# A hybrid decoder layer on one core: the pairwise recurrence, scores and value products as products of the whole array

## The chip, the core and the metric

The kernel runs on one core of a Trainium2 chip. Its time is the device time of one execution in microseconds, and the median of three runs is given. TensorE is the matrix engine, VectorE and ScalarE the vector engines, POOL (GpSimd) and SP two more, of which SP issues most of the transfers here.

## What is computed

One layer for 512 tokens of width 2048 in float32. The token's vector is normalized and multiplied with `w_in` (7296 columns); three groups of heads work on the result, each is gated with a SiLU, and one output projection adds to the input. Cut to what matters:

```
proj = _rms(x, norm_g) @ w_in                    # split into pa, pb, pc
# A: 12 heads of 64, a recurrence over the tokens
sa    = einsum('bhvk,bhk->bhv', state, -kk_t)
state = state * w_t + sa * (kk_t * a_t) + v_t * k_t
y_t   = einsum('bhvk,bhk->bhv', state, r_t)
# B: trailing means over 2, 4, 8 and 16 tokens minus the token, then a 128 x 128 map
yb = einsum('bsgc,gcd->bsgd', mean - u, pool_w) * pool_scale * silu(pg)
# C: 12 heads of 64, stick-breaking attention, strictly causal
z = q k^T;  log_1m = log_sigmoid(-z);  w = exp(log_sigmoid(z) + sum of the later log_1m)
yc = (w @ v) * silu(gc)
out = x + concat(ya, yb, yc) @ w_out
```

## The kernel before

**Projections.** `w_in` is cut into 57 tiles of 128 columns (`tile_order`): one for the decay and rate inputs, then for each of six pairs of heads eight tiles (k, r, v, ga of the recurrence, cq, ck, cv, cg of the attention), then eight for the pooling. A float32 product is made of three in the faster format f32r, of high and low parts (`three`, L408): 16 blocks x 3 = 48 products of 128x128 by 512 tokens per tile, into one of two banks `pj`. The weights come in halves of a tile, are split by ScalarE (`wh`) and VectorE (`wl`), and VectorE evacuates the result (`u`). The first three tiles run while the input arrives (`first`). The output projection at the end has 4 x 16 x 4 x 3 = 768 products (`oacc`).

**Small work in between.** All else is written as generators (`rwkv`, `attention`, `pooling`). After each big product `pump` lets those go on whose inputs are ready by a clock that `Pace` keeps while the program is built. `need(..., tag, margin)` gives that time. So the order on TensorE is fixed beforehand, and a wrong estimate becomes a wait. On VectorE, ScalarE and POOL the operations run in program order, weights and evacuations being put ahead (L426, L447).

**The recurrence** (`rwkv`, L506) treats two heads, one in the upper and one in the lower 64 rows, in eight chunks of 64 tokens. A pair waits until the pair before is done (L558). Then come the products inside the chunks (`gm`, L581 to L593, 64 rows of one head at a time), a triangular solve on VectorE by way of DRAM (L598 to L635), two visits of 32-row products (`q`) that complete the inverse `lt`, and the chunk loop from L687:

- `w`: two products of 128 rows and 64 columns, one for each head; VectorE copies the result to `wsb` and makes the decayed state `se`.
- `y`: two products of 64x64 (L702); `u`: two of 64x64 with `lt` (L705); VectorE copies u into `uv`.
- `s`: two products with `bkt`, then VectorE's update of `uv` for the next chunk with `se`; `y` again with `rx`, and ScalarE copies y out.

These are plain float32 products, and each stands as two records in the trace. Banks of PSUM are dealt out by kind: two for `pj`, three `g`, three `c`.

**The attention** (`attention`, L739) makes the scores `z` of a head in four blocks. In each block one product of 128 rows (high and low part of q against the high part of k) is followed by one of 64 rows (`klo`, L778). ScalarE, VectorE and POOL make the weights `w` of it, TensorE transposes them (`wT`), and four products per head, 64 columns wide, multiply with the values (`o`, L831). Decay and rate (`dec`, `av`, L519 to L525) are also a product of 128 rows and one of 64.

**Pooling** (L839) waits with its product until the last pair's recurrence and attention are through (L859), and the output projection takes the branches in the order recurrence, attention, pooling (`order`, L939).

Of the kernel before, what the change touches and what calls it, by code (L numbers as in the profile page):

```python
# [8 lines left out]
F32 = mybir.dt.float32  # L9
# [4 lines left out]
P = 128  # L14
# [38 lines left out]
BANKS = {"pj": 2, "g": 3, "c": 3}  # L53
# [150 lines left out]
def hybrid_trunk_kernel(ctx: ExitStack, tc: tile.TileContext, x, xT, w_in, w_out, vecs, consts, up_w, pool_w, out, tap=None):  # L204
# [15 lines left out]
    tp = ctx.enter_context(tc.tile_pool(name="tp", bufs=14))  # L220
# [57 lines left out]

    hh = [hp.tile([P, T], F32R, tag=f"hh{k}", name=f"hh{k}") for k in range(KT)]
# [14 lines left out]
    for pl, tag, parts in ((ap, "q2", 1), (ap, "k2", 1), (ap, "w3", 1), (rp, "bk", 2), (rp, "bkt", 2), (rp, "rx", 2),  # L294
                           (rp, "uv", 2), (rp, "amr", 3), (ap, "wt", 2)):
        xt = pl.tile([P, parts, T], F32, tag=tag, name=name("x"))
# [209 lines left out]
    def rwkv(p):  # L506
# [13 lines left out]
        mm(dec, upl[lo, 0:P], wd2[lo, :], False, True)  # L520
# [4 lines left out]
        mm(av, upl[hi, P:2 * P], ad2[hi, :], False, True)  # L525
# [35 lines left out]
        amr = rp.tile([P, NC_, 3, C], F32, tag="amr", name=name("amr"))  # L561
        for h, s in ((0, lo), (1, hi)):
# [7 lines left out]
        dve.tensor_tensor(amr[:, :, 2, :], r3, e[:, :, 1:], ALU.mult)  # L570
# [7 lines left out]
        lt = rp.tile([P, NC_, C], F32, tag="lt", name=name("lt"))  # L578
        ms = strict.rearrange("p (o t) -> p o t", o=1)
        mi = incl.rearrange("p (o t) -> p o t", o=1)  # L580
        for half in range(2):  # L581
            cs = slice(4 * half, 4 * half + 4)
            for h, s, other in quad:
                yield need(*([amr, bk] if half == 0 and h == 0 else []), tag="g")
# [6 lines left out]
                dve.tensor_tensor(lt[s, cs, :], g4[s, :, 0, :], ms[s].to_broadcast([HD, 4, C]), ALU.mult)  # L591
# [6 lines left out]
        for h in range(2):  # L598
            for b in range(2):
                r0 = h * HD + b * B  # L600
                dma(out=s1v[:, :, h, b, :], in_=lt[r0:r0 + B, :, b * B:(b + 1) * B])
# [30 lines left out]
        for h in range(2):  # L632
            for b in range(2):
                r0 = h * HD + b * B
                dma(out=lt[r0:r0 + B, :, b * B:(b + 1) * B], in_=s2v[:, :, h, b, :])  # L635
# [23 lines left out]
        xt = tmp("xt")  # L659
        dve.transpose(xt, lt.rearrange("p c t -> p (c t)"))  # L660
# [391 lines left out]
```

## Time and profile before

| | us |
|---|---|
| median of 3 runs | 1089.75 (1088.41 to 1089.97) |
| the profiled execution | 1089.68 |
| its span, first to last instruction | 1088.0 |
| TensorE busy | 1066.2 (98%) |
| VectorE busy | 737.6 (68%) |
| ScalarE busy | 427.8 (39%) |
| POOL busy | 143.1 (13%) |

In the rows PE is TensorE's product, DVE is VectorE, ACT is ScalarE. Products are pipelined: one begins before the one ahead of it has ended, so what one costs is read from start to start and not from its own length. A tile's name stands without its number, as out<-in. Ahead of a product's sizes stand the rows and columns of the array that it uses (128*128 is the whole of it).

### The profile page before, as it was taken

The page shows a single profiled execution, that of the slowest core. Times are in us where ns is not written, and L with a number is a line of the kernel's source. Part 1 is how long each engine was busy: PE and PEld are TensorE (multiplying, and loading weights), DVE is VectorE, ACT ScalarE, POOL GpSimd, SP SyncE. Part 2 cuts the span into 40 slices and gives each one's busy share as a digit, 9 for nine tenths or more (in the row PEclk, how much of TensorE's full clock was granted, in tenths as well). Part 3 has the DMA queues.
Part 4 walks back from the last instruction along what each step waited for, and adds up shares of the span by engine and source line. Part 5 has one row for each costly group of instructions (what it writes and reads, how often), then busy time and mean ns, then how long its engine had stood idle before and what let it go on. Part 6 is the DMA issues. An engine that isn't in the chain of part 4 may idle for free.

```text
span 1088.0 us, 14731 instructions
## 1 busy us (share of the span) xinstructions
PE 1066.2 (98%) x5552; PEld 801.3 (74%) x5552; DVE 737.6 (68%) x1596; ACT 427.8 (39%) x670; POOL 143.1 (13%) x208
## 2 busy tenths in 40 slices
PE   9998999999999999999999999999999999999998
PEld 7877766687666877668766787667776677888887
DVE  6266978759787797778877799777986457223232
ACT  6453525235353354334543345524443235111111
POOL 0031113101132011210211102210021111000000
PEclk9999999999999999899999999999999999999999
DMA  9513231132211321113221132112221125444232
GB/s 329 204 63 105 80 93 40 56 92 84 84 48 51 107 85 66 58 59 97 86 76 39 64 115 77 61 58 84 100 78 55 48 94 163 149 154 137 96 137 75
DMA packets 58185, 101.92 MB, mean 94 GB/s; under 512 B 29312, under 2 KB 30720, under 8 KB 58112
## 3 DMA queue, kind: packets, MB, share of 16 engines
q1 hardware_dynamic: 58112, 100.96, 28.2%
q8 instruction: 44, 0.72, 0.3%
q14 instruction: 29, 0.24, 0.1%
HBM read 95.17 MB, written 5.77 MB: 93 GB/s over the span
## 4 chain that ended last, share of the span: by engine, by line
PE 80%; DVE 10%; issue 4%; ACT 2%; DMA 2%; POOL 2%; SPq 0%; POOLq 0%; DVEq 0%; ACTq 0%
PE pj L350 45%; PE oacc L350 15%; PE first L350 3%; PE o L350 2%; PE z L350 2%; DVE w L198 2%; DVE wl L198 2%; PE gm L350 2%; PE y L350 2%; PE w L350 2%; PE wT L354 1%; DVE xblk L198 1%; PE u L350 1%; POOL e L198 1%; PE s L350 1%
## 5 line engine op out<-in xcount | busy, mean ns | idle before, releaser
L350 PE MATMUL pj<-hl,wh 128*128 128x512 f32 x864 | 349.0, 404 | 0.0
L350 PE MATMUL pj<-hh,wh 128*128 128x512 f32 x864 | 347.9, 403 | 1.0 <-DVE u L198 0.8
L350 PE MATMUL pj<-hh,wl 128*128 128x512 f32 x864 | 347.6, 402 | 0.0
L198 DVE TENSOR_TENSOR wl<-raw,wh 128x1024 fp32r<-128x1024 f32 x140 | 172.1, 1229 | 168.6 <-ACT wh L198 162.8
L198 ACT CAST wh<-raw 128x1024 fp32r<-128x1024 f32 x140 | 147.0, 1050 | 312.7 <-PE pj L350 187.5
L350 PEld LDWEIGHTS pj<-hh,wh 128*128 128x128 f32 x864 | 163.1, 189 | 38.0 <-issue 4.4
L350 PEld LDWEIGHTS pj<-hh,wl 128*128 128x128 f32 x864 | 163.2, 189 | 35.4 <-issue 0.4
L350 PEld LDWEIGHTS pj<-hl,wh 128*128 128x128 f32 x864 | 163.1, 189 | 35.5 <-issue 1.2
L350 PE MATMUL oacc<-wl,yh 128*128 128x512 f32 x256 | 100.1, 391 | 0.8 <-DVE wl L198 0.8
L350 PE MATMUL oacc<-wh,yl 128*128 128x512 f32 x256 | 99.6, 389 | 0.0
L350 PE MATMUL oacc<-wh,yh 128*128 128x512 f32 x256 | 99.6, 389 | 0.0
L198 POOL TENSOR_SCALAR e<-e 128x512 f32<-128x512 f32 x28 | 49.0, 1749 | 327.9 <-ACT e L198 327.6
L198 POOL TENSOR_TENSOR d<-u 128x512 f32<-128x512 f32 x25 | 34.2, 1370 | 230.9 <-DVE u L198 148.6
L350 PEld LDWEIGHTS oacc<-wl,yh 128*128 128x128 f32 x256 | 48.0, 188 | 11.5 <-DVE wl L198 1.3
L350 PEld LDWEIGHTS oacc<-wh,yl 128*128 128x128 f32 x256 | 48.1, 188 | 10.0 <-issue 0.2
L350 PEld LDWEIGHTS oacc<-wh,yh 128*128 128x128 f32 x256 | 48.0, 188 | 10.0
L198 DVE TENSOR_TENSOR xblk<-xblk,pr 128x60 f32<-128x60 f32 (+8 forms) x180 | 44.5, 247 | 4.1
L198 ACT ACTIVATE e<-e 128x512 f32<-128x512 f32 x50 | 31.4, 629 | 39.1 <-POOL e L198 38.8
L198 DVE TENSOR_TENSOR_SCAN w<-kon,n 128x512 f32<-128x512 f32 (+3 forms) x48 | 39.3, 841 | 6.6 <-POOL n L198 6.5
L198 DVE TENSOR_TENSOR pr<-xblk,nblk 128x60 f32<-128x60 f32 (+8 forms) x180 | 38.7, 215 | 4.4
L198 DVE TENSOR_TENSOR u<-pj,rstd 128x512 f32<-128x512 f32 x50 | 34.3, 686 | 8.3 <-PE pj L350 7.9
L198 ACT ACTIVATE n<-n 128x512 f32<-128x512 f32 (+1 forms) x72 | 38.9, 557 | 1.3
(195 smaller groups left out, 1262.7 us busy)
## 6 DMA issues: line engine op xcount, KB each, us to landing
raw<-in_w_in SPq DMA_DIRECT2D x108, 512.0 KB, 3.4
raw<-in_w_out SPq DMA_DIRECT2D x32, 512.0 KB, 3.4
xs<-in_x SPq DMA_DIRECT2D x8, 512.0 KB, 4.7
xr<-in_x SPq DMA_DIRECT2D x16, 256.0 KB, 5.3
out<-xr SPq DMA_DIRECT2D x16, 256.0 KB, 3.2
fr<-in_w_in SPq DMA_DIRECT2D x12, 256.0 KB, 7.4
nblk<-s SPq DMA_DIRECT2D x24, 128.0 KB, 4.9
x<-in_xT SPq DMA_DIRECT2D x5, 512.0 KB, 7.4
```

Source lines behind the costliest of these rows:

```text
L198: return call(*args, **kw)
L350: pe.matmul(o, lhsT, rhs, start=start, stop=stop)
L354: pe.transpose(o, src, ident)
```

## The change

Every product of the recurrence becomes one of the whole array: `amr` gets four columns per chunk (two for each head) and `lt` two, and the halves of the other head are set to zero, so that both heads go in one product and the wanted halves are picked out behind it. The copy of `w` is then two copies, y of four chunks gathers in a bank of its own, and `se` moves from VectorE to POOL. Scores, decay and rate use 128 rows throughout; for the scores POOL makes `kl2`, the low part of k twice. The value products of both heads of a pair are made side by side in one bank. Pooling doesn't wait any more, and the output projection takes pair 5 last. `tp` has 13 buffers instead of 14.

```diff
-BANKS = {"pj": 2, "g": 3, "c": 3}
+BANKS = {"pj": 2, "g": 3, "c": 2, "y": 1}
+Y_ORDER = [0, 1, 2, 3, 4, 10, 11, 12, 13, 14, 6, 7, 8, 9, 5, 15]
...
-            c = max(4 * max(n, 64) / 2400.0, 0.1) * (0.6 if m <= 64 or rhs.shape[0] <= 64 else 1.0)
+            c = max(4 * max(n, 64) / 2400.0, 0.214 if m > 64 else 0.1) * (0.6 if m <= 64 or rhs.shape[0] <= 64 else 1.0)
...
-        mm(dec, upl[lo, 0:P], wd2[lo, :], False, True)
+        mm(dec, upl[:, 0:P], wd2, False, True)
...
-        for h, s in ((0, lo), (1, hi)):
+        for h, s, other in quad:
+            pool.memset(amr[other, :, h, :], 0.0)
...
-        dve.tensor_tensor(amr[:, :, 2, :], r3, e[:, :, 1:], ALU.mult)
+        dve.tensor_tensor(amr[lo, :, 2, :], r3[lo], e[lo, :, 1:], ALU.mult)
+        pool.tensor_tensor(amr[hi, :, 3, :], r3[hi], e[hi, :, 1:], ALU.mult)
...
-                    rhs = amr[s, cc, 0:3:2, :] if h == 0 else amr[s, cc, 1:3, :]
-                    mm(g[:, j * P:(j + 1) * P], bk[s, cc, :, :], rhs)
+                    mm(g[:, j * P:(j + 1) * P], bk[:, cc, :, :], amr[:, cc, h:4:2, :])
...
-            yield need(amr, uv, tag="c", margin=TIGHT)
-            wps = cb("w")
-            for h, s, o in quad:
-                mm(wps[s, 0:C], amr[:, cc, h, :], uv[:, cc, h, :])
+            yield need(amr_flat, uv, tag="c", margin=TIGHT)
+            wus = cb("wus")
+            wps, ups, sps = wus[:, 0:P], wus[:, P:P + C], wus[:, 2 * P:3 * P]
+            mm(wps, amr[:, cc, 0:2, :], uv[:, cc, :, :])
             wsb = rp.tile([P, C], F32, tag="wsb", bufs=2, name=name("wsb"))
-            dve.tensor_copy(out=wsb, in_=wps[:, 0:C])
+            dve.tensor_copy(out=wsb[lo, :], in_=wps[lo, 0:C])
+            dve.tensor_copy(out=wsb[hi, :], in_=wps[hi, C:P])
...
-                    dve.tensor_scalar(se[s, :], uv[s, cc, h, :], ec[s, cc:cc + 1], None, ALU.mult)
-            yield need(wsb, lt, tag="c", margin=TIGHT)
...
-                mm(yps[s, 0:C], uv[s, cc, h, :], amr[s, cc, 2, :], True, False)
...
-                mm(ups[s, 0:C], lt[s, cc, :], wsb[s, :])
...
+                    pool.tensor_scalar(se[s, :], uv[s, cc, h, :], ec[s, cc:cc + 1], None, ALU.mult)
+            yield need(wsb, lt, tag="y" if cc % 4 == 0 else None, margin=TIGHT)
+            mm(ups, lt[:, cc, :, :], wsb)
...
+            mm(yps, uv[:, cc, :, :], amr[:, cc, 2:4, :], True, False)
+            dve.tensor_copy(out=uv[lo, cc, 0, :], in_=ups[lo, :])
+            dve.tensor_copy(out=uv[hi, cc, 1, :], in_=ups[hi, :])
+            yield need(uv, margin=TIGHT + 0.1)
...
-                    mm(sps[s, 0:C], bkt[:, cc, h * HD:(h + 1) * HD], uv[:, cc, h, :])
+                mm(sps, bkt[:, cc, :], uv[:, cc, :, :])
...
+            mm(yps, uv[:, cc, :, :], rx[:, cc, :, :], False, True)
...
+            kl2 = ap.tile([P, T], F32R, tag="kl2", name=name("kl2"))
+            pool.tensor_copy(out=kl2[s, :], in_=klo[s, :])
+            pool.tensor_copy(out=kl2[other, :], in_=klo[s, :])
...
-                    mm(z[:, off:off + (i + 1) * P], q2[s, i * P:(i + 1) * P], klo[s, 0:(i + 1) * P], False, True)
+                    mm(z[:, off:off + (i + 1) * P], q2[:, i * P:(i + 1) * P], kl2[:, 0:(i + 1) * P], False, True)
...
-            for j in range(4):
-                mm(o[s, j * P:T], vt[:, j, s], wt[:, pos[j]:pos[j] + T - j * P], j == 0, j == 3)
...
+            for j in js:
+                for h, s in ((0, lo), (1, hi)):
+                    mm(o[s, j * P:T], vt[:, j, s], parts[h][:, pos[j]], j == 0, j == 2)
...
-        while ("pg", g) not in got or not done.get(("gn", NPAIR - 1)) or not done.get(("att", NPAIR - 1)):
+        while ("pg", g) not in got:
...
+    for h, s, other in quad:
+        pool.memset(amr[other, :, 2 + h, :], 0.0)
+        pool.memset(lt[s, :, 1 - h, :], 0.0)
...
-    while len(tasks) > 1:
-        pump(True)
...
-        k = order[i]
-        while 6 <= k < 10 and tasks:
+        k = Y_ORDER[i]
+        while not done.get(ready[k]):
             pump(True)
```

## Rows read from the trace of the kernel before

**Rows 1.** Busy us (instructions) of PE, PEld, DVE, ACT, POOL; clock, DMA, GB/s.

```profile
42.00:908.00 866.00, 851.19 (x4619) 624.40 (x4617) 660.95 (x1502) 366.11 (x594) 137.06 (x199) 0.99 0.24 76
485.00:615.00 130.00, 128.77 (x722) 93.94 (x720) 104.42 (x240) 55.52 (x93) 20.24 (x30) 1.00 0.24 75
```

**Rows 2.** Chain of waits (start, us, what), and TensorE's timeline at the first output product.

```profile
920.99 163.28 PE oacc L350 x719
...
908.00 0.39 PE L350 MATMUL oacc<-wh,yh 128*128 128x512 f32 x1
```

**Rows 3.** Timeline of TensorE (start, us, instruction): a visit of u.

```profile
575.50 0.40 PE L350 MATMUL pj<-hh,wh 128*128 128x512 f32 x1
575.83 0.33 PE L350 MATMUL u<-wsb,lt 64*64 64x64 f32 x4
...
576.42 0.40 PE L350 MATMUL pj<-hh,wl 128*128 128x512 f32 x1
```

**Rows 4.** The same view: a visit of s and y, and the second big product behind.

```profile
854.11 0.34 PE L350 MATMUL s<-uv,bkt 128*64 128x64 f32 x4
854.27 0.29 PE L350 MATMUL y<-rx,uv 128*64 128x64 f32 x4
...
854.83 0.40 PE L350 MATMUL pj<-hh,wl 128*128 128x512 f32 x1
```

**Rows 5.** The same view: four transposes, and the two big products behind.

```profile
544.25 0.60 PE L354 MATMUL wT<-kon,w 128*128 128x128 f32 x4
544.60 0.47 PE L350 MATMUL pj<-hl,wh 128*128 128x512 f32 x1
544.91 0.39 PE L350 MATMUL pj<-hh,wl 128*128 128x512 f32 x1
```

**Rows 6.** The same view: a pooling product, and the second big product behind.

```profile
885.59 1.02 PE L350 MATMUL po<-pd,pw 128*128 128x512 f32 x2
...
886.68 0.40 PE L350 MATMUL pj<-hh,wl 128*128 128x512 f32 x1
```

**Rows 7.** The same view: the eight score products of a head.

```profile
656.50 0.40 PE L350 MATMUL z<-k,q 128*128 128x512 f32 x1
656.83 0.50 PE L350 MATMUL z<-klo,q 64*128 64x512 f32 x1
...
659.46 0.39 PE L350 MATMUL pj<-hh,wh 128*128 128x512 f32 x1
```

**Rows 8.** The same view: the decay's two products.

```profile
567.36 0.42 PE L350 MATMUL dec<-wd,sh 128*128 128x512 f32 x1
567.71 0.49 PE L350 MATMUL dec<-wd,sl 64*128 64x512 f32 x1
568.13 0.50 PE L350 MATMUL pj<-hh,wh 128*128 128x512 f32 x1
```

**Rows 9.** Chain of waits: first products of pair 3, and of pair 4.

```profile
485.31 1.64 PE gm L350 x16
488.54 1.08 PE gm L350 x8
...
615.15 1.64 PE gm L350 x16
```

**Rows 10.** Timeline of TensorE: the value products of a head.

```profile
553.02 2.37 PE L350 MATMUL o<-wt,vt 128*64 128x512 f32 x8
```

**Rows 11.** The same view: a visit of 32-row products.

```profile
547.29 0.69 PE L350 MATMUL q<-xt,lt 32*32 32x32 f32 x32
```

**Rows 12.** VectorE's groups of 485 to 615 us: count, busy us, mean ns, idle before.

```profile
L198 DVE TENSOR_SCALAR se<-uv,ec 64x64 f32<-64x64 f32 x14 | 3.5, 249 | 0.4
L198 DVE COPY wsb<-w 128x64 f32<-128x64 f32 x8 | 1.8, 223 | 3.6 <-PE w L350 3.4
```

**Rows 13.** The page's costliest groups: POOL.

```profile
L198 POOL TENSOR_SCALAR e<-e 128x512 f32<-128x512 f32 x28 | 49.0, 1749 | 327.9 <-ACT e L198 327.6
```

**Rows 14.** TensorE's waits by releaser: total us, times, longest.

```profile
PE w L350 <- DVE uv L198: 4.2, 5, 1.2
```

More of the change, by code (lines that the diff above doesn't have):

```diff
@@ L583, in rwkv @@
             for h, s, other in quad:
-                yield need(*([amr, bk] if half == 0 and h == 0 else []), tag="g")
+                yield need(*([amr_flat, bk] if half == 0 and h == 0 else []), tag="g")
                 g = gb("gm")
@@ L656, in rwkv @@
         yield soon(lt)
-        xt = tmp("xt")
-        dve.transpose(xt, lt.rearrange("p c t -> p (c t)"))
-        xt3 = xt.rearrange("p (c t) -> p c t", t=C)
+        xt = tmp("xt", NC_ * B)
+        xt3 = xt.rearrange("p (c t) -> p c t", t=B)
+        for h in range(2):
+            dve.transpose(xt3[h * HD:h * HD + B], lt[h * HD:h * HD + B, :, h, 0:B])
         yield need(xt, tag="g")
@@ L812, in attention @@
                 act.copy(out=vt, in_=vps.rearrange("p (j c) -> p j c", j=4))
-            wt = ap.tile([P, 1280], F32, tag="wt", name=name("wt"))
-            pos = {}
-            off = 0
-            for js, width in (((0,), 512), ((1, 3), 512), ((2,), 256)):
-                yield need(*blocks.values(), tag="g", margin=MARGIN + 2.0)
+        o = None
+        for js, width in (((0,), 512), ((1, 3), 512), ((2,), 256)):
+            parts = []
+            for h in range(2):
+                yield need(*head[h].values(), tag="g", margin=MARGIN + 2.0)
                 tps = gb("wT")
-                o2 = 0
+                pos = {}
+                off = 0
                 for j in js:
-                    pos[j] = off + o2
+                    pos[j] = slice(off, off + T - j * P)
                     for i in range(j, 4):
-                        transpose(tps[:, o2:o2 + P], blocks[(i, j)])
-                        o2 += P
-                dst = wt[:, off:off + width]
-                (dve.tensor_copy if js[0] != 1 else act.copy)(out=dst, in_=tps[:, 0:width])
-                off += width
-            yield need(wt, vt, tag="g")
-            o = gb("o")
-            for j in range(4):
-                mm(o[s, j * P:T], vt[:, j, s], wt[:, pos[j]:pos[j] + T - j * P], j == 0, j == 3)
-            while ("cg", p) not in got:
-                yield None
-            y = yt[Y_TILE[("c", p)]]
-            dve.tensor_tensor(y[s, :], o[s, :], y[s, :], ALU.mult)
+                        transpose(tps[:, off:off + P], head[h][(i, j)])
+                        off += P
+                home = {(0, 0): "q2", (0, 1): "k2", (1, 0): "kl2", (2, 0): "q2", (2, 1): "k2"}.get((js[0], h))
+                wt = ap.tile([P, T], F32, tag=home, name=name("wt"))[:, 0:width] if home else tmp("wt", width)
+                (dve.tensor_copy if h == 0 else act.copy)(out=wt, in_=tps[:, 0:width])
+                parts.append(wt)
+            yield need(*parts, vt, tag="g" if o is None else None)
+            if o is None:
+                o = gb("o")
+            for j in js:
+                for h, s in ((0, lo), (1, hi)):
+                    mm(o[s, j * P:T], vt[:, j, s], parts[h][:, pos[j]], j == 0, j == 2)
+        while ("cg", p) not in got:
+            yield None
+        y = yt[Y_TILE[("c", p)]]
+        dve.tensor_tensor(y, o, y, ALU.mult)
         done[("att", p)] = True
@@ L900, in finish @@
             got[(kind, i)] = u
-    first = [cb("first") for _ in range(NFIRST)]
+    first = [bank(("c", "c", "y")[n], "first") for n in range(NFIRST)]
     for kq in range(KT // KQ):
@@ L967, in hybrid_trunk_kernel @@
                 for i in (2 * i2, 2 * i2 + 1):
[L968 removed]
+                    k = Y_ORDER[i]
                     sl = slice((i % 2) * 512, (i % 2) * 512 + 512)
```

66 lines of the change are left out of this document (32 added, 34 removed).

## The prediction

> **What bounds the kernel now.** I read the table of busy time by stretch first. From 42 to 908 us, where all but the first three input columns are projected, TensorE is busy 851.2 of 866 us at a granted clock of 0.99, and VectorE 661 [rows 1]. Waiting is 14.8 us there. So TensorE's own work is the bound, and the question is what that work is. Next the chain of waits: 719 output products in a row took 163.28 us, 0.227 us each [rows 2]. The 54 projected columns have 54 x 16 x 3 = 2592 such products, 588.6 us of the 851.2. The other 262.6 us are the small products that are let in between them.
>
> Then the timeline of TensorE around single visits of small products. I price a visit from the start of the big product ahead of it to the start of the second one behind it, less 2 x 0.227; the ends of products overlap, their starts don't. One fp32 product stands as two records.
> - A visit of four u records: 576.42 - 575.50 - 0.454 = 0.47 us [rows 3]. The lead-in is 0.33 instead of 0.23, and the big product behind has the next one 0.33 after it.
> - s and y together, eight records: 0.72 plus the same lead-in of 0.33, less 0.454, is 0.60 [rows 4]. Four more records cost 0.13, so the first four cost some 0.16 and the remaining 0.3 is the edge of the visit. Four records of 64 columns one after the other at two cycles a column would be 0.21; 0.13 means that the two heads, on different columns of the array, run together.
> - Four 128x128 transposes: 0.66 + 0.23 - 0.454 = 0.44, that is 0.11 each and no edge [rows 5]. One fp32 product 128x128 by 512 columns, two records: 1.09 + 0.23 - 0.454 = 0.87, that is 0.43 each, just the two cycles a column, and no edge either [rows 6].
> - Eight score products, alternately of 128 and 64 rows: 2.96 + 0.24 - 0.454 = 2.75 us for 2560 columns, which stream in 1.07 [rows 7]. Eight changes of shape, about 0.2 each. The decay product has the same: the 64-row half begins 0.35 after the 128-row one and is followed after 0.42, where 0.23 is normal [rows 8].
>
> So the edge is not paid for small fp32 products but each time the shape of the array (rows x columns, the figure ahead of the sizes) changes: some 0.15 to 0.2 us per change. [...]
>
> **The change, part by part.** First what the recurrence costs now, as the remainder of the 262.6 us. Scores 12 x 2.75 = 33.0. The first products of the recurrence (gm): per pair one visit of 16 records at 1.64 and two of 8 at 1.08 [rows 9], each with 0.2 of edge, 4.4 a pair, 26.5. Value products (o): 2.30 of streaming (1280 columns at four cycles are 2.13) and an edge of 0.2, 2.5 per head, 30 [rows 10]. Decay and rate products 12 x 0.88 = 10.5. Transposes 216 x 0.11 = 23.8. The 32-row products (q) 0.69 and edges, 0.9 a visit, 12 visits, 10.9 [rows 11]. 72 other full-shape products at 0.235, 16.9. Pooling 2.6. Together 154, which leaves 108 for the recurrence, 2.25 us a chunk. At its best a chunk has 0.47 + 0.60 + 0.60 = 1.67 or 80 in all; many visits are split in two and pay the edge twice.
> - *Recurrence in full shape.* 5 x 48 - 6 = 234 products in place of 468 in quadrants or halves. Each has two records of 128x128; the rows of that size cost 0.11, so 0.22 a product and 52 to 54 in all. The u product has only 64 moving columns and may cost half: down to 47. Edge: none. Saved: 55 by the remainder, 27 by the best visits; I take 50, near the remainder, which counts what really ran.
> - *Scores with 128 rows.* Eight products at 0.227, 0.174, 0.12 and (as the transposes) 0.11, two of each, 1.27 in place of 2.75: 12 x 1.48 = 18 saved. Decay and rate: 12 x 0.42 = 5 saved.
> - *gm in full shape.* 96 products at 0.22 are 21 in place of 26.5: 5 saved.
> - *Paired value products.* The visits become three per pair, of both heads, with an edge of about 0.3 each. If the heads overlap as in [rows 4], in order of issue the second record of the first head runs with the first of the second: three quarters of the serial time, (1280 x 2 x 4 cycles = 4.27) to 3.1; with edges 4.1 a pair, 24.5 in place of 30, 5 saved. Bounds: no overlap, 1 lost; perfect overlap, 11 saved.
> - *VectorE and POOL.* The copy wsb becomes two (8 x 0.22 more a pair), se goes to POOL (14 x 0.25 less) [rows 12]. VectorE falls from 104.4 to some 102 us a pair. POOL gets se, two copies of klo per head, half of r times E and two clears of half a tile: by its row of 1.75 us for 512 columns [rows 13] at most 4 x 1.75 + 1.75 + 14 x 0.3 + 1.2, or 14 us a pair on top of 20 of 130. It stays mostly idle.
> - *Waits.* The saved edges also covered the hand-over to VectorE. There are 3 x 48 - 6 = 138 hand-overs; late by 0.2 each they cost 28, not late at all 0. At present the longest group of them costs 4.2 us in all [rows 14]. I take 7.
> - *At no cost.* Pooling at once and the last pair last: no product of TensorE is added, and 719 output products follow without a break now [rows 2], so there is no hole to close. They are cover: pair 5 is needed only 14 x 12 x 0.227 = 38 us into the output projection, and if pair 5 comes later than that the rest is paid in full. Ten loads of x instead of nine and four clears of zeros lie in the first 42 us; 0 to 1 us, taken as 0.
>
> The sum: 50 + 18 + 5 + 5 + 5 = 83 saved, 7 given back, 76 in all. The profiled execution took 1089.68 us (span 1088.0 and 1.7 around it), which is the median of 1089.75 within 0.1. So 1089.7 - 83 + 7 = 1013.7, and as u may be cheaper than 0.22 I say 1012.
>
> **The rivals.**
> *A, VectorE becomes the bound.* It is busy 104.4 of the 130 us of a pair, 80% [rows 1]; with 102 of 116 it would be 88%, in strict order, and what it is late with (weights, evacuations) stops TensorE. For: of its 25.6 idle us a pair some come from waiting in order, which a faster TensorE doesn't remove. Against: TensorE waits for it only a few us in all [rows 14]. If 20 of the 25.6 stay, a pair takes 122 and not 116: 6 x 6 = 36 more, of which the waits above hold a part, about 1045.
> *B, the edge belongs to the visit, not to the shape.* Then 144 visits of the recurrence and 18 of gm still pay 0.2 each, 32 us, and the packing of [rows 4] is lost as well: about 1044. Transposes and the pooling product, small or fp32 and without edge, speak against it [rows 5, 6]. [...]
> *C, slower: the chain of a pair grows.* From one pair's gm to the next's are 129.84 us [rows 9], just what eight projected columns take, and the pairs follow one another without overlap there. The change puts se on POOL, in order, behind operations of 1.75 us [rows 13]; VectorE's update of uv waits for it, and everything queued behind that update on VectorE (wl, the evacuations) with it. Pair 5's gm would come at 615 + 130 = 745 and its end by 875 to 885 if the chain stays as long; TensorE, whose output projection begins at 908 now [rows 2], would need it at 908 - 83 + 38 = 863. So an unchanged chain costs 12 to 22, inside the range. To eat the whole gain it must be 10 us longer a pair, 1.3 us a chunk: from there on it is slower, at 2 us a chunk 1089.7 - 76 + 6 x 16 + 15 = 1125. Against: the chunk has some 7 us, and se is needed only at its end.
> *D, no change:* the products are not made full-shape after all or waits take all. The edits leave little room for that.
>
> **How the numbers follow.** Forecast 1012, as worked out: 0.66, with 992 to 1028 as its own range (u at half, 6; perfect overlap, 6; no waits, 7; against it 21 more waits or 7 of value products). A 0.21, B 0.06, C 0.04, D 0.03. All but C and D are faster. For 8 in 10 the range reaches from 992 into most of A: 992 to 1042. Faster by over 0.2% (about what a measurement of this kernel can tell from no change): 0.93; within: 0.03; slower: 0.04.
>
> **What would show it.** Right, if small fp32 products stand as 128*128 in the timeline and the big ones around them keep 0.23 ahead and some 0.3 behind; if the eight scores take some 1.3 us; if TensorE's busy time from 42 us to the first output product falls from 851 to about 770 and VectorE's stays near 655. Value products of two heads should start within each other's time. A shows as TensorE waiting for wl, u or uv for over 30 us; B as lead-ins of 0.33 ahead of 128*128 records; C as a hole in TensorE ahead of the last two of sixteen blocks of the first output columns. The forecast is wrong if a 128x128 fp32 product with 128 columns costs much more than 0.22, or if the remainder of 108 holds something else than the recurrence.

## The result, and the profile after

The changed kernel takes 1100.1 us, median of four runs (1098.6 to 1101.2), the kernel before beside it 1089.9: a ratio of 1.0088, 95% interval 1.0059 to 1.0116. It is slower by 0.9%; forecast were 1012 us. The profiled execution spans 1096.9 us.

The page of the profile after: span, and the busy time of the engines with their shares.

```profile
span 1096.9 us, 13928 instructions
...
PE 1023.6 (93%) x5084; PEld 812.4 (74%) x5084; DVE 726.8 (66%) x1554; ACT 427.8 (39%) x652; POOL 234.7 (21%) x338
```

The table by stretch, whose columns are those of [rows 1], for the time from the first product behind the three input columns to the first output product, and for two windows of the length of a pair.

```profile
40.00:917.00 877.00, 809.57 (x4150) 636.30 (x4149) 650.43 (x1460) 366.22 (x578) 226.11 (x323) 0.97 0.23 75
485.00:615.00 130.00, 122.04 (x634) 94.95 (x633) 101.19 (x231) 53.59 (x85) 34.78 (x50) 0.97 0.23 75
615.00:745.00 130.00, 117.21 (x620) 92.16 (x619) 99.44 (x229) 54.45 (x87) 34.34 (x50) 0.97 0.21 68
```

TensorE is busy 809.6 us where it was 851.2 [rows 1], and yet the stretch is longer, 877 instead of 866: 67 us of it are idle, and the clock fell from 0.99 to 0.97. The output projection takes 180 us in both. So all of the loss lies ahead of it, and the work did become less. Who is waited for stands in TensorE's waits (engine, line, releaser: us in all, times, longest):

```profile
PE q L361 <- DVE xt L201: 21.0, 5, 7.8
PE wus L361 <- DVE uv L201: 12.8, 11, 2.3
PE wus L361 <- DVE wsb L201: 10.1, 10, 2.6
PE q L361 <- DVE w L201: 5.8, 3, 2.8
PE gm L361 <- issue: 5.1, 1, 5.1
```

Nothing like the first line stood in the waits before; their longest group was the 4.2 us of [rows 14]. The wait in pair 4, first in the timeline of TensorE (start, us, instruction, in brackets the idle time ahead of it and its releaser):

```profile
647.25 0.39 PE L361 MATMUL pj<-hh,wl 128*128 128x512 f32 x1
651.94 0.24 PE L361 MATMUL q<-xt,lt 32*32 32x32 f32 x2 [4.30 <-DVE xt L201]
652.11 0.56 PE L361 MATMUL pj<-hh,wh 128*128 128x512 f32 x1
652.47 0.63 PE L361 MATMUL pj<-hl,wh 128*128 128x512 f32 x1
652.89 0.63 PE L361 MATMUL pj<-hh,wl 128*128 128x512 f32 x1
653.32 0.63 PE L361 MATMUL pj<-hh,wh 128*128 128x512 f32 x1
```

and the same wait in the chain of waits (start, us, what):

```profile
612.49 5.96 DMA xblk<-s
...
641.71 0.59 DVE cq L201
642.30 1.14 DVE wl L201
643.90 5.77 DMA s<-xblk
649.68 1.75 DMA lt<-s
651.45 0.44 DVE xt L201
651.94 0.24 PE q L361 x2
```

The 32-row products wait for the triangular solve: 40 us from the load of `xblk` to `q`, in which VectorE's small steps stand between weights (`wl`, 1.14 us) and attention work, and two trips through DRAM. Before, TensorE went from a pair's last `gm` to its `q` in 55.5 us in pairs 2 to 5, with 210 big products between them, and found `xt` ready 2.5 to 2.9 us earlier. In pair 3 of the kernel before, `xt` is done at 544.67, and `q` starts at 547.29 [rows 11]:

```profile
543.97 0.70 DVE L198 STREAM_TRANSPOSE xt<-lt 128x512 f32<-128x512 f32 x1
```

Now the order has 190 to 195 big products there in pairs 3 to 5, and `q` comes after 49.8 to 52.5 us only because it waits. The solve itself, from the last `gm` to `xt`, took 53 us in these pairs before; now it takes 50 to 52 to the first half of `xt`, which is made in two, and 51 to 54 to the whole. It is TensorE that became quicker. The idle time at `q`, as a group of the table by line (count, busy us and mean ns, then idle before, by releaser):

```profile
L361 PE MATMUL q<-xt,lt 32*32 32x32 f32 x192 | 6.2, 214 | 26.3 <-DVE xt L201 21.0 <-DVE w L201 5.3
```

The 5.3 us are of pairs 1 and 2 and aren't the solve's: there `xt` had been ready for 3.4 us, and `q` waited for VectorE's step `w` of the attention, which reads scores from a bank. That it is the bank which `q` needs is likely, not shown.

The chains of the window 615 to 745 us, before and after, in shares of the chain by line:

```profile
by line: PE pj L350 68.7%; PE z L350 3.9%; PE o L350 3.5%; PE gm L350 3.2%; PE y L350 2.6%; PE w L350 2.6%; DVE w L198 2.1%; PE wT L354 1.7%; PE u L350 1.4%; PE s L350 1.2%; POOL e L198 1.2%; PE q L350 1.0%; POOL w L198 0.9%; issue 0.8%; PE
```

```profile
by line: PE pj L361 27.3%; DVE wl L201 6.1%; DVE w L201 6.0%; issue 5.7%; DVE pr L201 5.4%; DVE xblk L201 4.9%; DMA xblk<-s 4.6%; DMA s<-xblk 4.4%; PE gm L361 2.9%; PE wus L361 2.5%; POOL se L201 1.9%; POOL e L201 1.9%; DVE c L201 1.8%; DVE
```

Big products made up two thirds of the chain before and make up a quarter now; the solve (`pr`, `xblk`, `s`) and VectorE's other work have come in.

The idle time isn't all. In the timeline above the big products stand 0.43 us apart behind the wait, where 0.23 is usual. The table by stretch shows the granted clock there, in a stretch almost without waits, and in 17 us around the longest wait (7.8 us, ended at 158.6):

```profile
652.00:655.60 3.60, 3.60 (x12) 2.90 (x12) 3.33 (x6) 0.00 (x0) 0.00 (x0) 0.56 0.47 155
133.00:151.00 18.00, 17.18 (x76) 13.35 (x75) 17.17 (x50) 8.99 (x16) 5.97 (x9) 1.00 0.16 60
154.20:171.20 17.00, 10.78 (x91) 9.06 (x92) 7.23 (x15) 4.78 (x9) 2.27 (x5) 0.50 0.26 76
```

In the traces of before and after every stretch is granted either 1.00 or 0.50, and half clock here means a stretch at 0.50, where the big products stand 0.43 us apart instead of 0.23. In after, every stretch at half clock ahead of the output projection begins in or just behind a wait of 2.5 us or more, and there were 47.8 us of it (10.2 before). Not every wait has one behind it: of the 13 waits of 1.5 us or more, eight have. From here on the stretch up to the first output product is split so: idle time ahead of TensorE's instructions; half of the time at half clock, as lost (an estimate: 0.43 us for 0.23 would be 47%); and the rest, which is TensorE's work at full clock. Idle time that lies at half clock is counted in both of the first two; in after that is 8.1 us, in before none. Without it the work of after is 789.6 and its loss 19.8. One experiment below (se on VectorE, first version) has no such split, since its profiled execution fell into a disturbed run. In us:

| kernel | median | stretch | idle | lost to half clock | rest | idle + rest |
|---|---|---|---|---|---|---|
| before | 1089.9 | 865.9 | 14.8 | 5.1 | 846.0 | 860.8 |
| after | 1100.1 | 876.9 | 67.4 | 23.9 | 785.6 | 853.0 |

TensorE's work fell by 56 to 60 (the first with idle time at half clock taken out); idle time rose by 52.6, and the loss to the clock by 15 to 19.

### The profile page after: what moved, and what is told of

Same layout as the page of the kernel before. It is cut to its first block, busy times and chain, and to the rows that moved or that the text cites. A ratio compares the mean times of both kernels' runs of the same rounds, so it can differ in the third digit from the quotient of the medians.

```text
span 1096.9 us, 13928 instructions
## 1 busy us (share of the span) xinstructions
PE 1023.6 (93%) x5084; PEld 812.4 (74%) x5084; DVE 726.8 (66%) x1554; ACT 427.8 (39%) x652; POOL 234.7 (21%) x338
## 4 chain that ended last, share of the span: by engine, by line
PE 49%; DVE 26%; DMA 10%; POOL 5%; issue 4%; ACT 4%; SPq 1%; POOLq 0%; DVEq 0%; ACTq 0%
PE pj L361 23%; PE oacc L361 15%; DVE wl L201 5%; DVE w L201 3%; DVE xblk L201 3%; DVE pr L201 3%; PE wus L361 3%; DMA s<-xblk 3%; DMA xs<-in_x 2%; PE gm L361 2%; POOL e L201 2%; PE o L361 2%; DMA xblk<-s 2%; DVE u L201 1%; PE y L361 1%
## 5 line engine op out<-in xcount | busy, mean ns | idle before, releaser
L201 DVE TENSOR_TENSOR wl<-raw,wh 128x1024 fp32r<-128x1024 f32 x140 | 176.7, 1262 | 181.5 <-ACT wh L201 180.4
L201 POOL CAST kl<-klo 64x512 fp32r<-64x512 f32 x24 | 18.7, 778 | 236.4 <-DVE klo L201 190.8
L201 POOL TENSOR_SCALAR se<-uv,ec 64x64 f32<-64x64 f32 x84 | 49.8, 593 | 83.9 <-DVE uv L201 79.0
L361 PEld LDWEIGHTS oacc<-wh,yl 128*128 128x128 f32 x256 | 48.0, 188 | 10.2 <-issue 0.2
L361 PEld LDWEIGHTS oacc<-wh,yh 128*128 128x128 f32 x256 | 48.0, 188 | 10.1
L201 DVE TENSOR_TENSOR xblk<-xblk,pr 128x60 f32<-128x60 f32 (+8 forms) x180 | 40.4, 224 | 4.2
```

The costliest lines, as they stand in the source:

```text
L201: return call(*args, **kw)
L361: pe.matmul(o, lhsT, rhs, start=start, stop=stop)
```

## The experiments

Theory P: the order on TensorE is fixed by the planner's clock. The planner charges VectorE 0.065 us and 1.04 ns a column, where [rows 12] have 0.22 for 64 columns; about 240 such operations a pair [rows 1]. Before, TensorE was late too, by its uncharged changes of shape (some 0.2 us each in the scores, an estimate from [rows 7]), and so the two agreed. TensorE's saved time is then waited for at the solve, and the waits cost clock besides. The rivals: se on POOL, the copies kl2, the output order, a longer chain of the pair (rival C). All times below have their ratio to the kernel before on the same chip; the table at the end splits them.

**The 32-row products planned 6 us later.**

```diff
-        yield need(xt, tag="g")
+        yield need(xt, tag="g", margin=MARGIN + 6.0)
```

> The changed kernel with only the first 32-row products (q) planned 6 us later. In the changed kernel TensorE waits 26 us there in six pairs, and its clock is at half behind most of these waits. P: these waits go, and some 10 us of half clock with them: 1060 to 1075. C: as much is waited for elsewhere, at the chunks or for pair 5: 1090 to 1105.

1081.0 us, ratio 0.9896 (0.9871 to 0.9921): 19 us less than after, by one number of the plan, and less of a gain than theory P's 1060 to 1075. Idle time at `q` fell from 26.3 to 6.2, a single wait in pair 0, third line of the waits:

```profile
PE wus L361 <- DVE uv L201: 7.2, 10, 1.7
PE vps L365 <- DVE w L201: 6.3, 5, 2.3
PE q L361 <- DVE xt L201: 6.2, 1, 6.2
PE pj L361 <- DVE wl L201: 6.0, 6, 3.3
```

But idle time as a whole fell by 18 only, to 49: other waits for VectorE took its place in part. The number moves more than `q`, since the whole order behind it is planned anew: in pair 1 `q` now starts 36 us after `xt` is ready.

**The same, 3 us** (`MARGIN + 3.0`).

> The kernel after with the first 32-row products planned 3 us later instead of 6. Theory P: of the eleven or so waits there the longest were 4 to 8 us, so 3 us take about half of their length, and the clock behind the longest stays halved: between 1081 and 1100, nearest 1088. If the place and not the length decides (rival: 6 us gained because they moved other work to a better place), the time isn't between the two: below 1080 or at 1100 and above.

1083.6, ratio 0.9900 (0.9870 to 0.9931): between the two, as theory P said, but by its interval not to be told apart from 6 us.

**The same 6 us in the kernel before.**

> Control: the kernel before with its first 32-row products planned 6 us later, as in the run of the changed kernel that gained. In the kernel before TensorE waits 0.4 us there in all. If late planning only removes waits there is nothing to gain: 1088 to 1096 (a longer chain of a pair, 6 us, may cost a little at the end). If it helps by itself, whatever the products: 1070 to 1080.

1117.9, ratio 1.0245 (1.0220 to 1.0270), far over the 1088 to 1096 expected. There is nothing to gain where `q` doesn't wait, and a pair becomes longer: from gm to gm 136 to 150 us instead of 130 to 136. The old order finishes small work before the output projection: the last projected product starts at 915.1 and the first output product at 928.2, so 13 us of the longer chain stand alone there. The rest is waits at the transposes `wT` (11.4 us) and clock (14.3 us lost instead of 5.1). Rival C's price is real.

**Only the new scores, decay and rate in the kernel before** (with kl2 on POOL).

```diff
...
-                    mm(z[:, off:off + (i + 1) * P], q2[s, i * P:(i + 1) * P], klo[s, 0:(i + 1) * P], False, True)
+                    mm(z[:, off:off + (i + 1) * P], q2[:, i * P:(i + 1) * P], kl2[:, 0:(i + 1) * P], False, True)
```

> The kernel before with one part of the change alone: scores, decay and rate products of 128 rows (POOL makes the second copy of klo). Theory of the array's shape: eight scores fall from 2.75 to some 1.3 us and the decay's two products from 0.88 to 0.46, 18 + 5 = 23 us less TensorE work; the chunk loop still pays its changes of shape, so TensorE seldom arrives early: 1065 to 1075. Theory P taken strictly: any TensorE time saved turns into waits: 1080 to 1095.

1123.7, ratio 1.0294 (1.0263 to 1.0325). TensorE's work fell from 846.0 to 822.5: 23.5 us, or 21 with idle time at half clock taken out, where the prediction's two terms are 18 + 5. And the kernel is some 32 us slower, outside both expectations, with these waits:

```profile
PE q L350 <- DVE xt L198: 18.6, 5, 5.5
PE z L350 <- DVE uv L198: 5.1, 3, 1.9
PE s L350 <- DVE uv L198: 4.9, 5, 2.0
```

71.7 us at half clock went with them. The saving came within 2 us of the forecast, and its sign in the time was wrong.

**VectorE charged what it takes, in the kernel after:** 0.155 and 0.095 us instead of 0.065.

```diff
-        return 0.065 + n * 0.00104
+        return 0.155 + n * 0.00104
```

> The changed kernel with one constant of the planner's clock raised: a VectorE operation is counted with 0.155 us beside its elements and not 0.065. The traces give that: a copy of 64 columns out of PSUM takes 0.22, 512 columns 0.69, 1024 columns 1.22. Theory P (the plan): the work saved on TensorE is really saved, but the order on TensorE is fixed by a clock that counts VectorE some 0.09 us short per operation, about 20 us a pair; before, the unplanned changes of shape on TensorE made up for it, now TensorE arrives too early. Then waits on TensorE fall from 73 us to under 40, the granted clock rises from 0.978 to 0.99 and the time to 1020 to 1050. Theory C (the chain): a pair's chain of 128 us itself bounds, wherever TensorE waits for it; then the waits only move and the time stays within 1% of 1100.

> The kernel after with VectorE's fixed cost in the plan at 0.095 us instead of 0.065, a third of the step to 0.155 that made a pair's chain 165 us long and cost 24 us. Theory P with rival C's price (waits shrink, but a pair's chain grows): the chain grows to some 135 to 140 us a pair, short enough for the output projection to cover it, and the waits ahead of the 32-row products shrink by a part: 1080 to 1095. If every step of that kind lengthens the chain beyond its gain: 1100 to 1112.

With 0.155: 1124.2, ratio 1.0298 (1.0256 to 1.0339), so the remedy that follows from theory P as it stood fell. The plan counts a result as ready 0.12 us after its end, so that along a chain of dependent steps it wasn't short by the whole 0.09; by the code 0.155 charges such a chain too much, though no run separates this. The first output product comes at 833, but a pair now takes up to 181 us from gm to gm, the last small product of pair 5 comes at 982.7, and TensorE stands in the output projection, much of it at half clock. The stretch around it, and the wait that stands in it, 13.5 us long:

```profile
857.00:960.00 103.00, 67.94 (x318) 52.79 (x318) 53.82 (x164) 12.24 (x19) 10.34 (x22) 0.67 0.20 62
```

```profile
PE q L361 <- DVE xt L201: 14.2, 2, 13.5
```

This wait follows 168 = 14 x 12 output products: it is rival C's hole ahead of the last two blocks, made by the plan and not by POOL. With 0.095: 1077.1, ratio 0.9882 (0.9861 to 0.9903); the waits at `q<-xt` are down to 4.0 and pairs take 134 to 141 us, which the output projection still covers. It is faster than the 1080 to 1095 expected.

**The chunk loop planned later** (`TIGHT` 0.05 to 0.4).

> The changed kernel with the products of the chunk loop planned 0.35 us later each (TIGHT 0.4 in place of 0.05). The changed kernel waits some 26 us at them, and shorter waits hide in the tail of the big product ahead. P: two thirds of these go: 1065 to 1085; the chain of a pair grows by 8 x 3 x 0.35 = 8 us, which is not waited for. C: the longer chain is paid in full: 1100 to 1125.

1102.9, ratio 1.0105 (1.0057 to 1.0152), not different from after and against theory P's 1065 to 1085. Waits in the chunk loop fell; those at `q` stayed (20.7 of 26.3), and 16.4 came up at `z`.

**Sixteen big products of no use ahead of the first visit of q in each pair**, to keep TensorE busy.

```diff
+        for _ in range(16):
+            pe.matmul(q1, hh[0][:, 0:P], hl[0], start=True, stop=True)
```

> The changed kernel with 16 extra big products (3.6 us at full clock, their result is overwritten) ahead of each first group of 32-row products, six times 3.6 = 22 us of work that nobody needs. The waits there were 2.5 to 7.8 us, 26 in all, and the clock was at half behind each for 3.4 to 17 us. If the idle itself brings the clock down: the waits fall to some 6 us, half clock in the stretch from 48 to about 20 us, which is 14 us less lost; the filling costs 2 to 3 us more than the waits it replaces; 1085 to 1093, faster with more work. If the clock has another cause (the kind of products, VectorE's or POOL's activity): 1100 to 1105.

1113.5, ratio 1.0216 (1.0183 to 1.0248), outside both ranges. The filling added 24.4 us of work and itself waited 9.2 us for VectorE's `w`, which fits the bank above; half clock fell from 47.8 to 41.0 only, and the order behind the filling changed. This tells nothing on what the clock alone costs.

**All small work before the output projection again**, and pooling held back.

```diff
...
+    while tasks:
+        pump(True)
     yh, yl = {}, {}
```

> The kernel after, with the pooling product held back until the last pair is through, and all small work finished before the output projection begins, as in the kernel before; the order of the inputs in the output projection stays as changed. If the early pooling and the late last pair bring nothing here, because pair 5 is through long before the output projection (theory P): 1100, within 3 us. If they cover the end of the chain, as the change intends: 1105 to 1115, with idle time of TensorE ahead of the first output product.

1100.1, ratio 1.0060 (1.0044 to 1.0076): as after. In the kernel after, all but two of TensorE's small products are done by the first output product anyway, and the new order covers nothing. In the versions with `q` 6 us later it covers some 11 us: there the last small product starts that long after the first output product.

**se on VectorE again**, in the kernel after and in the one with `q` 6 us later.

```diff
-                    pool.tensor_scalar(se[s, :], uv[s, cc, h, :], ec[s, cc:cc + 1], None, ALU.mult)
+                    dve.tensor_scalar(se[s, :], uv[s, cc, h, :], ec[s, cc:cc + 1], None, ALU.mult)
```

> The changed kernel with se back on VectorE (84 operations of some 0.25 us, 21 us in all, against 0.59 each on POOL). If POOL's slow se lies on a pair's chain: chunks shorten, 1085 to 1095. If VectorE's load is what makes TensorE wait: longer waits at q and the chunks, 1105 to 1120. If neither: within 0.5% of 1100.

> The kernel after with two edits: the first 32-row products are planned 6 us later, and se is made on VectorE again. Theory P (TensorE's order is fixed beforehand, what is saved turns into waits ahead of the solve's products and in the chunk loop, and the clock is halved behind each longer wait): the two edits act in different places, 19 us at the 32-row products and 5 us in the chunk loop, so the gains add up: 1076, with 1072 to 1080. Rival S (each of them only shifts a pair's chain, and one shift takes the place of the other): no faster than the first edit alone, 1081 to 1085.

1094.6, ratio 1.0023 (1.0005 to 1.0041), and 1078.3, ratio 0.9861 (0.9845 to 0.9877): 5 and 3 us less. Only the first is clear of the noise (ratios 1.0088 and 1.0023; in the second, 0.9896 and 0.9861, the intervals overlap), and with the old scores, below, the place of se makes no difference (1073.5 and 1073.8). Moving se to POOL was a small loss in the kernel as changed; more isn't shown.

**The old 64-row scores in the kernel after**, without kl2; the same with `q` 6 us later.

> The changed kernel with scores, decay and rate products of 64 rows again, as before: some 23 us more TensorE work. Theory P: these changes of shape lie between the first products and the 32-row products of a pair, and delayed TensorE just where it now waits. So the waits at q and the slow clock behind them fall by about as much: 1085 to 1103, no slower than the changed kernel. If TensorE's work alone counted: 1120 to 1125.

> The kernel after with the 32-row products planned 6 us later, and with the scores, decay and rate of the kernel before (64-row second products). Without the late planning these old products made the kernel after 15 us faster although they cost TensorE 21 us more. Theory P: they did so only by making TensorE reach the 32-row products later; with those planned late there is nothing left to gain, and the 21 us count at least in part: 1085 to 1102, slower than the 1081 of the late planning alone. Rival K (the scores' new form is bad in itself, by its copies on POOL or by the work it puts in the way of the chain): the 15 us are gained again, 1066 to 1072.

1085.1, ratio 0.9942 (0.9920 to 0.9964), and 1073.5, ratio 0.9811 (0.9787 to 0.9835). In both TensorE does some 20 us more than with the new scores, and both are faster, by 15 and 8 us. The second is against theory P's forecast and near rival K's: it was not only by the place of `q`.

**The old shapes with everything else of the new scores**, kl2 and its waits, so that all engines have the same instructions in the same order as after; the same with `q` 6 us later.

```diff
...
-                    mm(z[:, off:off + (i + 1) * P], q2[:, i * P:(i + 1) * P], kl2[:, 0:(i + 1) * P], False, True)
+                    mm(z[:, off:off + (i + 1) * P], q2[s, i * P:(i + 1) * P], kl2[s, 0:(i + 1) * P], False, True)
```

> The kernel after with only the shapes of the second products of scores, decay and rate changed to 64 rows; the copies kl2 on POOL stay and are awaited, and every engine has the same instructions in the same order. TensorE has some 21 us more to do. Theory P (in a fixed order the time saved is waited for and the clock falls behind the waits): no slower than after, 1085 to 1100, with waits 20 to 27 us shorter. Rival K (the copies and their place in the order make the new scores slow): the 21 us come on top, at least in part, 1108 to 1121.

> The same shapes in the version with the 32-row products planned 6 us later (1081); again the same instructions in the same order on every engine. Theory P: 1073 to 1083. Rival K: 1090 to 1102.

1117.7, ratio 1.0251 (1.0217 to 1.0285), and 1084.2, ratio 0.9948 (0.9930 to 0.9966). In the fixed order the work is 15.7 and 19.0 us more, and idle time 12.6 and 13.4 us less: 70 to 80% of what the new shapes save is waited for. That is theory P's waits, measured. What is left would be 3 and 6 us; measured are 18 and 3, the second just above theory P's range. The 15 us over in the first are clock: 81.9 us at half clock instead of 47.8, for the most part behind waits at the same places (behind the one at `q` in pair 3, 20.5 us instead of 6.8). The time is the one that rival K gave and not theory P's, and kl2 with the order that comes with it does cost (below); but by the split, work on top is only a small part of what is paid here. The clock is seen in a window of a pair, beside the row of after above:

```profile
615.00:745.00 130.00, 119.35 (x586) 91.82 (x586) 92.95 (x215) 52.34 (x83) 33.45 (x49) 0.93 0.22 69
```

**Why kl2 costs 33 us (1117.7 against 1085.1) with the same products.** The plan charges 1.77 us a copy, the trace has 0.78. With the true charge:

```diff
+            if f == "tensor_copy":
+                return 0.06 + n * 0.0014
             return 0.08 + n * (0.0028 if f == "tensor_scalar" else 0.0033)
```

> The kernel after with one number of the plan changed: a copy of 512 columns on POOL is charged 0.78 us, as the trace has it, instead of 1.77. The program's operations are the same. If the order that the charge leads to is what makes the new scores slow: 1075 to 1092, and the waits ahead of the 32-row products fall from 26 to below 12. If the copies themselves are slow for the chain: 1095 to 1105, with those waits unchanged.

1106.1, ratio 1.0124 (1.0105 to 1.0143), in neither range. Waits at `q` fall to 15.5, but 11.7 come up at `z`, behind VectorE's solve, and 68 us are at half clock. In this run one more true charge, in a plan that is wrong elsewhere, only moved the wait.

**The best of these together:** old scores, `q` 6 us later, se on VectorE; and the same with the new scores and kl2 on ScalarE.

> 64-row scores without the copies kl2, the 32-row products planned 6 us later, and se on VectorE: the version that the runs so far point to. If se's place in the chunk loop counts as it did in the other two versions (3 to 5 us): 1068 to 1071. If the chunk loop's waits are covered already: 1073.

> The kernel after with the 32-row products planned 6 us later, se on VectorE and the copies kl2 on ScalarE: the version of 1073.8 with the new scores instead of the old ones, 19 us less for TensorE. If two thirds of what is saved is waited for, as at the same order, and the clock stays as it is: 1066 to 1070. If everything is waited for: 1074 to 1079. If the copies on ScalarE hold up the gates and weights behind them: above 1080.

1073.8, ratio 0.9851 (0.9834 to 0.9868), and 1079.6, ratio 0.9887 (0.9871 to 0.9903). The first has no wait at `q` in its list; its longest groups of the chunk loop, and the window of a pair:

```profile
PE wus L361 <- DVE wsb L201: 5.3, 10, 0.9
PE wus L361 <- DVE uv L201: 5.1, 10, 1.5
```

```profile
615.00:745.00 130.00, 126.71 (x655) 96.38 (x655) 108.42 (x250) 55.40 (x89) 23.23 (x35) 0.99 0.23 74
```

The second has 18.8 us less to do and is 6 us slower, just above what its expectation gave for all of it being waited for.

The versions on which the conclusions rest, split as above:

| kernel | median | stretch | idle | lost to half clock | rest | idle + rest |
|---|---|---|---|---|---|---|
| before | 1089.9 | 865.9 | 14.8 | 5.1 | 846.0 | 860.8 |
| before, new scores | 1123.7 | 900.0 | 41.7 | 35.8 | 822.5 | 864.2 |
| before, q 6 later | 1117.9 | 887.7 | 26.3 | 14.3 | 847.0 | 873.3 |
| after | 1100.1 | 876.9 | 67.4 | 23.9 | 785.6 | 853.0 |
| same order, 64 rows | 1117.7 | 897.0 | 54.8 | 41.0 | 801.3 | 856.1 |
| old scores | 1085.1 | 864.1 | 40.3 | 17.1 | 806.8 | 847.1 |
| kl2 charged 0.78 | 1106.1 | 883.5 | 61.2 | 34.1 | 788.1 | 849.3 |
| VectorE charged 0.095 | 1077.1 | 850.9 | 53.6 | 15.4 | 781.9 | 835.5 |
| q 3 later | 1083.6 | 861.9 | 54.6 | 27.3 | 780.0 | 834.6 |
| q 6 later | 1081.0 | 853.3 | 49.0 | 18.8 | 785.5 | 834.5 |
| q 6 later, se on VectorE | 1078.3 | 850.0 | 47.4 | 13.7 | 788.9 | 836.3 |
| same order, 64 rows, q 6 later | 1084.2 | 855.5 | 35.6 | 15.4 | 804.5 | 840.1 |
| old scores, q 6 later | 1073.5 | 847.9 | 31.6 | 11.9 | 804.3 | 835.9 |
| old scores, q 6 later, se on VectorE | 1073.8 | 845.1 | 33.1 | 6.8 | 805.3 | 838.4 |
| new scores, kl2 on ScalarE, q 6 later | 1079.6 | 852.6 | 49.1 | 17.1 | 786.5 | 835.6 |

Each split is of one profiled execution, and executions of one kernel differ: the four of "same order, 64 rows" took 1113.1 to 1121.3 us at granted clocks of 0.972 to 0.958. Where `q` is planned 6 us later the output projection takes 185 to 186 us instead of 180; four small products, a wait of 4.1 us for VectorE and 3.4 to 6.8 us at half clock lie in it. In the eight versions from the charge of 0.095 on, all planned so that `q` comes later than in after, TensorE's work lies between 780 and 805 us, and work and idle time together are the same within 6: less work is more waiting, and something other than TensorE's work seems to set the pace. What then tells them apart is mostly the column of the half clock.

## Why the prediction was wrong, step by step

- **The bound was read rightly, its distance wasn't.** TensorE's work was the bound before. But the solve behind it was only 2.5 to 2.9 us off in pairs 2 to 5, and 0.1 us in pairs 0 and 1. That is to be read in the trace before, as the time from the end of `xt` to the start of `q`; the prediction looked only at what waits there were.
- **The sum.** Forecast was 76 us less, measured is a stretch longer by 11. Of the 87 us between, some 46 are waits (52.6 against 7), 23 to 27 are work that was not saved, and 15 to 19 are clock.
- **Step "Waits": the one that failed.** It priced the 138 hand-overs in the chunk loop with 0 to 28 us, took 7, and left out `q`; idle time rose by 52.6. The chunk loop's waits are 23 us (7.5 + 10.1 + 5.6), inside its bounds; `q` has 26.3. Its reasoning, that a saved edge no longer covers a hand-over, holds for every hand-over in a fixed order, not just for those in the loop that is edited.
- **The clock was no term at all.** 15 to 19 us more were lost by it. The trace of before had it: its 10.2 us at half clock stand behind two waits, of 0.9 and 1.2 us. A wait's price is its length and what the products behind it lose.
- **The saved work was 56 to 60 instead of 83.** The prices of single visits held: the eight scores take 688.50 to 689.76, 1.26 us (forecast 1.27),

```profile
688.50 0.39 PE L361 MATMUL z<-k,q 128*128 128x512 f32 x1
...
689.64 0.28 PE L361 MATMUL z<-kl,q 128*128 128x256 f32 x1
689.76 0.40 PE L361 MATMUL pj<-hl,wh 128*128 128x512 f32 x1
```

  a visit of u takes 0.23 to 0.36, mostly 0.28, less than its 0.47 [rows 3], and big products have 0.23 ahead of 128x128 records, so rival B is out. The 16 gm records are 1.79 and the 8 are 0.90 a visit, 3.6 a pair instead of 4.4, as forecast 5 us in all. The value products of two heads, where they stand together, are at the favourable bound: four records of 512 columns take 1.01 us from start to start of what follows,

```profile
713.47 1.08 PE L361 MATMUL o<-wt,vt 128*64 128x512 f32 x4
714.48 0.66 PE L365 MATMUL wT<-kon,w 128*128 128x128 f32 x4
```

  where two products one after the other would be 1.7 by [rows 6]: two heads run side by side. But in 8 of the 18 visits a product of the recurrence got in between the heads, and then each part takes as long, or nearly, as both heads together do:

```profile
564.53 1.07 PE L361 MATMUL o<-wt,vt 128*64 128x512 f32 x2
565.53 0.49 PE L361 MATMUL wus<-uv,bkt 128*128 128x128 f32 x2
565.86 0.39 PE L361 MATMUL y<-rx,uv 128*128 128x128 f32 x2
566.17 1.07 PE L361 MATMUL o<-wt,vt 128*64 128x512 f32 x2
567.17 0.50 PE L361 MATMUL pj<-hh,wl 128*128 128x512 f32 x1
```

  From start to start, the value products took 27.5 us in all before and take 22.1 now. So the forecast 5 us came, but by luck: from perfect overlap in ten visits and next to none in eight, not from a partial one in each. The prediction counts in cycles a column, and no run shows a cycle, only times: at 0.87 us for 512 columns [rows 6] its 2.13 us are 2.17 and its 4.27 are 4.35, and at 0.227 for 512 [rows 2] its 1.07 are 1.14.
- **Within it, the term of the recurrence was mis-sized.** With every product charged from start to start, waits left out, time at half clock halved, and what the big products beside it take over 0.227 added, the recurrence costs 98 us before and 67 after. That is 31 saved, near the prediction's lower bound of 27 (best visits) and not the 50 that it took: the remainder of 108 held some 10 us of something else, and the new products cost 67 instead of 53. "Edge: none" was not quite right, since the big product behind a visit has the next one 0.31 after it and not 0.23. By the same account scores, decay and rate fell by 18 (forecast 23), value products by 5 (5) and gm by 4 (5).
- **Rival A came nearest.** TensorE waits for VectorE 59 of the 67 us, and VectorE's share of the chain rose. Its mark as written isn't there, though: for `wl`, `u` and `uv` together TensorE waits some 17 us, not over 30; the rest is `xt`, `wsb` and `w`. Its price of 36 us lacked the clock. It also took VectorE's busy time for the measure; busy time fell (650 against 661 [rows 1]). What counts is the latency of one chain on VectorE, with its trips through DRAM, in the middle of other work.
- **Rival C** was slower, as it came, but not by its mechanism: the pair's chain didn't grow (gm to gm 121 to 137 us, on the mean 129; before 130 to 136, on the mean 132). Where the plan was stretched (0.155 us, above), its hole stood at the place that it gave.
- **"At no cost":** the output order was that, rightly, but also without worth, because pair 5's recurrence is through well ahead of the output projection in both kernels (its last `y` starts at 864 and 848 us, the first output product at 908 and 917). POOL's se was costed at 0.3 us each and takes 0.59 (columns: line, engine, form, count, then busy us and mean ns, then idle before):

```profile
L201 POOL TENSOR_SCALAR se<-uv,ec 64x64 f32<-64x64 f32 x84 | 49.8, 593 | 83.9 <-DVE uv L201 79.0 <-POOL se L201 0.2
L201 POOL CAST kl<-klo 64x512 fp32r<-64x512 f32 x24 | 18.7, 778 | 236.4 <-DVE klo L201 190.8 <-PE pj L361 30.6 <-PE z L361 14.1
```

What stays open: why half clock lasts longer in one version than in another behind waits of about the same length (47.8 and 81.9 us at the same order of instructions; a part may be chance, as the spread of the four executions says), and what in kl2's place in the order sends the small work to worse places. The runs show that they do, not by what rule. The new division of the banks, the 13 buffers of `tp` and the pairing of the value products, which changes the order of the attention, were not run alone.

## What to carry to other kernels

In a kernel whose order is fixed beforehand, work taken off the busiest engine is worth only as much as the next chain is behind it: for each hand-over read how long its input had been ready, since work saved ahead of it beyond that margin turns into waiting as long as the order stays. The idle share of the other engine doesn't tell it. A planner is tuned to the errors of all its charges together; who makes one kind of work cheaper has to move the margins of the long hand-overs with it, one by one, since a later plan also lengthens the chain and is paid where nothing covers its end. Compare versions by idle time, clock and work apart: the same order with another shape is the experiment that separates them.

## What the runs showed of the hardware

- Many waits of TensorE are followed by products at half clock: 0.43 us from start to start instead of 0.23, for 3.4 to 17.1 us at a stretch in after and up to 20.5 at the same order with 64 rows. It came behind waits of 0.9 and 1.2 us before and of 2.5 to 7.8 us after, but not behind every wait: three of 1.5 to 1.7 us in before have none behind them, and with kl2 charged 0.78 three of 2.7 to 2.8 us have none. Between the versions of the table, 5.1 to 41.0 us of the stretch went by it. In the rows above 0.50 was granted around the wait of 7.8 us and 1.00 in the 18 us ahead of it; what brings the clock down, no run shows.
- The small operation se, 64x64 with a scalar per row, took 0.59 us on POOL in after and 0.25 on VectorE before [rows 12].
- VectorE's copies and two-input operations show a fixed part of about 0.155 us, an estimate from two lengths: 0.22 for a copy of 64 columns [rows 12] and 0.69 for 512 in the timeline of after,

```profile
643.73 0.69 DVE L201 TENSOR_TENSOR bv<-bn,d 128x512 f32<-128x512 f32 x1
```

  so 1.04 ns a column and 0.155 besides. Two more lengths of before lie on that line: 0.42 for the copies of 256 columns and 1.22 for `wl` of 1024, where the line gives 0.42 and 1.22. Others take more: se is 0.249 for 64 columns [rows 12]. The plan's 0.065 is 0.09 short of the 0.155.
- Two products of 128 rows and 64 columns on different halves of the array's columns ran side by side at 512 columns too: 1.01 us for the pair where no other product stood between them, and 1.0 for each where products of the recurrence did.
